# Moving rows of rotated attention queries between partitions: 32 small transfers become 32 copies on ScalarE

## The chip, the cores and the metric

One core of a Trainium2 chip runs the whole program. TensorE (PE) multiplies and transposes, VectorE (DVE), ScalarE (ACT) and GpSimd (POOL) do the elementwise work, and SyncE (SP) issues most of the transfers (DMAs). Each engine runs its own instructions in order and waits for the others by semaphores. The metric is the device time of one execution in microseconds (us); lower is better.

## The reference

A trunk of two layers, each over 1024 tokens of width 1024. A layer is a normalisation with conditioning, one wide input projection, three groups of heads side by side (windowed attention, retention, gated linear attention), a gate on each, and one output projection that is added to x.

```python
h = rms_norm(x, pre_gain) * (1.0 + scale) + shift
proj = h @ w_in
(aq, ak, av, ag, rq, rk, rv, rg, gq, gk, gv, gg, ga) = jnp.split(proj, IN_SPLITS, axis=-1)
aq = apply_rotary(aq.reshape(B, S, ATTN_HEADS, HEAD_DIM), positions, rope_freq)
ak = apply_rotary(ak.reshape(B, S, ATTN_KV_HEADS, HEAD_DIM), positions, rope_freq)
a_out = sliding_window_attention(aq, ak, av, sinks) * jax.nn.silu(ag)
...
def apply_rotary(x, positions, inv_freq):
    ...
    x1, x2 = jnp.split(x.astype(jnp.float32), 2, axis=-1)
    out = jnp.concatenate([x1 * cos - x2 * sin, x2 * cos + x1 * sin], axis=-1)
```

The change concerns `aq` alone: 8 query heads of 64 numbers, each rotated as two halves of 32.

## The kernel before

**Matrix products.** Activations and weights are split into a high and a low part, and each projection is three passes over 8 blocks of 128 input columns, 24 matmuls for one PSUM tile. Weights come in blocks of 256 columns ("units") through five staging buffers `st`, are split by ACT, DVE and POOL into an arena, and are multiplied from there. Three PSUM banks (`mm`) serve the projections; five (`aux`) serve, in turn, everything else: scores, transposes, attention values.

**The order of the work.** PE runs in the order in which the program is written (`manual_schedule` for PE): while projections are emitted, a written-out clock `clk` and a table of latencies `L` decide after which matmul the next piece of a waiting job (scores, transposes, values) is put in. So PE always has projection matmuls to run while softmax and the like pass through the other engines. The instructions of the other engines and of the transfer queues are put in order by the framework, by its own estimates; exchanging an instruction there can move neighbours.

**Queries.** `attn_rot` is called four times in a layer: for half `hf` of the tokens (512 each) and for key head `g`. Each call projects transposed queries of four heads, so that features lie on partitions and 512 tokens in a row. Two PSUM tiles, c = 0 and 1, hold the first and the second rotary halves: 32 partitions for each head. DVE multiplies each by cosine and sine (L867, L868; the tables come from DRAM by `t<-tabS`), then forms u[0] and u[1] (L870, L871), the rotated first and second halves. For the scores a head's 64 features have to lie together, the first half right beside the second: ACT copies u[j] to q[j] whole (L874), and then, for each j and r, 32 partitions of the other tile are put over the wrong quarter of q[j] (L877). That last step changes partitions (to 0, 32, 64 or 96 from another of these), and is done by 32x512 transfers on SP's queue, SBUF to SBUF, 64 KB each: 4 in a call, 16 in a layer, 32 in all. They are seen as `t<-t` in the profile. Afterwards `split_later` splits q on ACT (L835) and DVE (L836) into `mx`, which PE multiplies with the keys `kT` (`attn_scores`).

**Softmax.** `attn_turn` brings scores from PSUM into `smx` by ACT (L145, the previous block) and DVE (L934, the current block under the causal mask), reduces (L936), takes exponentials on ACT (L939), the reciprocal on DVE (L942), and scales on POOL (L943). PE transposes `smx` (L176), ACT copies the transposes out (L145, `t<-aux`), POOL masks a second version (L954), and PE forms the values. ACT copies these out (L145 again, `t<-aux`), SP stores them to DRAM (`aoS<-t`), and once two blocks of tokens of a half are there they come back as `t<-aoS` for the gate (L1445).

In layer 0 the modulation of the next layer is computed beside this: DVE accumulates rows of `w_mod` (L367), each from its own staging buffer.

Of the kernel before, what the change touches and what calls it, by code (L numbers as in the profile page):

```python
# [13 lines left out]
AF = mybir.ActivationFunctionType  # L14
# [5 lines left out]
S = 1024  # L20
# [69 lines left out]
def trunk(ctx: ExitStack, tc: tile.TileContext, ins, cst, out):  # L90
    nc = tc.nc
    V, A, G, T = nc.vector, nc.scalar, nc.gpsimd, nc.tensor
# [16 lines left out]
    def t2(dt=F32):  # L109
        return gp.tile([P, 512], dt, tag="t2", name=nm("t2"), bufs=B2)  # L110
# [10 lines left out]
    def mm():  # L121
        return ps.tile([P, 512], F32, tag="mm", name=nm("mm"), bufs=MMB)
# [4 lines left out]
    def f(ap):  # L127
        return ap.bitcast(F32)
# [11 lines left out]
    def eng(k):  # L140
        return G if EN[k] == "G" else V

    def copy(k, dst, src):
        if EN[k] == "A":
            A.activation(dst, src, AF.Copy)  # L145
        else:
            V.tensor_copy(dst, src)

    def dma(k, dst, src):
        {"S": nc.sync, "A": A, "P": G}[EN[k]].dma_start(dst, src)  # L150

# [31 lines left out]
    def job(gen):  # L183
        jobs.append([clk[0], None, gen])
# [21 lines left out]
    def pump():  # L206
        moved = True
        while moved:
            moved = False
            for j in list(jobs):  # L210
                r = ready(j)
                if r is not None and r <= clk[0]:
                    step(j)
                    moved = True
                    break
# [251 lines left out]
    def load(l, name, first=None, kcs=range(KT // 2)):  # L467
# [116 lines left out]
    def pre(l, t, xt, early=False, soon=False):  # L584
# [9 lines left out]
        with ExitStack() as es:  # L594
# [99 lines left out]
    def mix_tile(dt=F32R):  # L694
        return gp.tile([P, 2, KT, P], dt, tag="mx", name=nm("mx"), bufs=2)
# [142 lines left out]
    def split_later(mq, q, name):  # L838
        yield lat("aq6", name[1])
        for j in range(2):  # L840
            split(mq[:, 0, j], mq[:, 1, j], q[j])
        flag(name, lat("aq2", name[1]))
# [13 lines left out]
    def attn_rot(l, hf, g, w_):  # L856


        sn, cs = t2(), t2()
        for s, d in ((0, sn), (1, cs)):  # L860
            nc.sync.dma_start(d.rearrange("p (s n) -> p s n", s=2),
                              tabS[2 * hf:2 * hf + 2, :, s, :].rearrange("s p n -> p s n"))
        u, w = [t2(), t2()], [t2(), t2()]
        for c in range(2):
            pm = mm()
            project_T(pm, l, hf, w_, c * P)
            V.tensor_tensor(u[c], pm, cs, ALU.mult)  # L867
            V.tensor_tensor(w[1 - c], pm, sn, ALU.mult)  # L868
            pump()
        V.tensor_tensor(u[0], u[0], w[0], ALU.subtract)  # L870
        V.tensor_tensor(u[1], u[1], w[1], ALU.add)  # L871
        q = w
        for j in range(2):
            A.activation(q[j], u[j], AF.Copy)  # L874
            for r in range(2):
                dst, src = 64 * r + 32 * (1 - j), 64 * r + 32 * j
                dma("qst", q[j][dst:dst + 32], u[1 - j][src:src + 32])  # L877
        mq = mix_tile().rearrange("p a k q -> p (a k q)").rearrange("p (a j n) -> p a j n", a=2, j=2)
        kv[(hf, g)] = mq
        job(split_later(mq, q, ("q", l, hf, g)))  # L880
# [46 lines left out]
    def attn_turn(l, held, sms):  # L927
        for t, n, sm, pss in sms:
            for r in range(2):
                pv = pss[r][:, 0:2 * n].rearrange("p (j c n) -> p j c n", j=2, n=P)  # L930
                sv = sm[:, r:4:2, 0:128]
                if t > 0:
                    copy("sprev", sv, pv[:, :, 0, :])
                V.copy_predicated(sv, curmask.unsqueeze(1).to_broadcast((P, 2, P)), pv[:, :, n // P - 1, :])  # L934
            mx = small(4)
            V.tensor_reduce(mx, sm, AX.X, ALU.max, negate=True)  # L936
            sums = small(4)
            for h in range(4):
                A.activation(sm[:, h, :], sm[:, h, :], AF.Exp, bias=mx[:, h:h + 1],  # L939
                             accum_out=sums[:, h:h + 1])  # L940
            rs = small(4)
            V.reciprocal(rs, sums)  # L942
            eng("pn").tensor_tensor(sm[:, :, 0:128], sm[:, :, 0:128], rs.unsqueeze(2).to_broadcast((P, 4, P)), ALU.mult)  # L943
        yield lat("aq3", l)
        for t, n, sm, pss in sms:
            pp = aux()
            for h in range(4):
                transp(pp[:, h * P:(h + 1) * P], sm[:, h, 0:128], ident)
            pf = t2()
            copy("pf0", pf, pp)  # L950
            parts = [(held[("vp", t)], pf)]
            if t > 0:
                pr = t2()
                G.affine_select(h4(pr), h4(pf), [[0, 4], [1, P]], ALU.is_ge, 0.0, base=0, channel_multiplier=-1)  # L954
                parts.append((held[("vd", t)], pr))
            held[("parts", t)] = parts
# [356 lines left out]
    def layer(l):  # L1313
# [140 lines left out]
        for hf in range(2):  # L1454
            for g in range(2):
                attn_rot(l, hf, g, unit(l, f"aq{g}"))
                pump()
                if hf:
                    load(l, ("o3", "ag1")[g])
# [46 lines left out]


B2, B1, BS, BST, MMB, SMB = 12, 8, 11, 5, 3, 6
EN = {"qst": "S", "smh": "S", "sml": "S", "sm0": "S", "sm1": "S", "lao": "S", "sao": "S", "lmix": "S", "ssg": "S", "lsg": "S", "ssr": "S", "lsr": "A", "lx": "S", "sx": "A", "lw": "S", "lwm": "S", "whi0": "V", "whi1": "A", "whi2": "A", "whi3": "A", "wlo0": "V", "wlo1": "G", "wlo2": "V", "wlo3": "G", "xn0": "V", "xn1": "V", "hlo0": "G", "hlo1": "V", "rot0": "V", "rot1": "V", "rdec": "V", "kslo": "V", "qslo": "V", "vlo": "G", "kT": "A", "qT": "A", "sprev": "A", "pn": "G", "pf0": "A", "aoc": "A", "hng": "V", "mh": "A", "gso": "V", "mg": "V", "mgl": "V", "rT": "A", "rv": "A", "gv": "A", "gk": "A", "ak0": "V", "ak1": "V", "ak2": "V", "ak3": "V", "kd0": "G", "kd1": "G", "kd2": "G", "kx1": "G", "kx2": "G", "kx3": "V", "kx4": "V", "qb": "G", "stx": "V"}
TURN = ("AV", "AV")  # L1510
L = {"tt1": 5.71, "tt2": 6.96, "tb1": 28.02, "tb2": 0.05, "pf3": 12.62, "pf1": 6.69, "pf2": 4.0, "mod1": 4.3, "mod2": 2.4, "mod3": 17.69, "mod4": 5.8, "mod5": 0.09, "mod6": 0.05, "pre1": 7.43, "kv1": 8.84, "kv2": 2.31, "aq1": 7.17, "aq7": 7.95, "ag1": 5.62, "aq2": 2.4, "aq6": 6.2, "aq3": 11.35, "aq4": 7.54, "aq5": 4.01, "hn1": 8.14, "hn2": 3.76, "gz1": 10.47, "gz2": 13.49, "gl1": 4.43, "gd3": 16.57, "gc1": 1.21, "gc2": 1.95, "gc3": 0.65, "gc4": 3.27, "gc6": 3.2, "gc5": 4.23, "rc1": 0.73, "rc2": 2.11, "rc3": 1.31, "rc4": 2.84, "fin1": 11.68, "lay1": 0.05, "mod2@1": 2.23, "mod3@1": 16.46, "mod5@1": 3.78, "mod6@1": 3.24, "pre1@1": 10.18, "kv1@1": 3.37, "kv2@1": 0.05, "aq1@1": 5.95, "aq7@1": 6.81, "ag1@1": 8.3, "aq2@1": 2.07, "aq6@1": 9.39, "aq3@1": 11.0, "aq4@1": 6.32, "aq5@1": 1.76, "hn1@1": 10.35, "hn2@1": 3.59, "gz1@1": 3.83, "gz2@1": 12.55, "gl1@1": 17.99, "gd3@1": 15.63, "gc1@1": 1.6, "gc2@1": 1.95, "gc3@1": 0.47, "gc4@1": 1.87, "gc6@1": 0.05, "gc5@1": 1.38, "rc1@1": 0.12, "rc2@1": 3.46, "rc3@1": 2.6, "rc4@1": 5.99, "fin1@1": 9.35, "lay1@1": 1.23, "gc7": 0.81, "gc7@1": 0.33, "tb0": 0.05, "mod7": 1.0, "mod7@1": 1.0}
CHUNK = 7
# [51 lines left out]
```

## Time and profile before

| | |
|---|---|
| time, median of 3 runs | 972.73 us (972.31 to 973.64) |
| profiled execution | 971.16 us, of it 969.4 us from its first to its last instruction |
| granted TensorE clock | 0.996 |
| PE | busy 951.3 us, 98% of the span |
| DVE, ACT, POOL | 640.2, 410.1, 272.5 us (66%, 42%, 28%) |
| first to last `L874` | 300.2 to 809.8 us: in layer 0 the four calls lie at 300 to 346, in layer 1 at 764 to 810 |

A row of the timeline gives the start in us, the duration, engine, line, operation, output and inputs, and how many instructions are merged; in brackets the engine's idle time before it and what ended it. SPq is the transfer queue of SyncE: the duration there is that of issuing, not of the transfer.

### The profile page before, as it was taken

How to read it: one execution, taken by the hardware profiler on the slowest of the kernel's cores; microseconds unless marked ns; L12 is line 12 of the kernel's file. 1: busy time of each engine (PE TensorE's matmuls, PEld its weight loads, DVE VectorE, ACT ScalarE, POOL GpSimd, SP SyncE). 2: the span in 40 equal slices, each digit the busy share in tenths (PEclk: the TensorE clock that was granted, in tenths of full speed). 3: DMA queues.
4: the chain of work that ended last, by engine and by line, in shares of the span. 5: the costliest groups of instructions: out<-in, count | busy, mean ns of one | idle time of the engine just before them, and what ended most of it. 6: DMA issues, size and time to landing. Idle time of an engine off the chain costs nothing.

```text
span 969.4 us, 18061 instructions
## 1 busy us (share of the span) xinstructions
PE 951.3 (98%) x6513; PEld 829.4 (86%) x6513; DVE 640.2 (66%) x1525; ACT 410.1 (42%) x1119; POOL 272.5 (28%) x323
## 2 busy tenths in 40 slices
PE   6999999999999999999999999999999999999997
PEld 1799999989998877878889999998999887777886
DVE  6886857777777777655586485686776577763332
ACT  2777312354422666622455531134652166761111
POOL 3243011533430344511242110144423034441000
PEclk9999999999999999999999999999999999999999
DMA  9943314624335355677455160253222333555871
GB/s 313 320 146 110 111 56 129 187 77 112 115 102 150 98 168 180 218 242 237 172 166 172 50 180 22 83 155 92 80 86 77 120 88 105 158 174 174 261 238 65
DMA packets 124293, 140.30 MB, mean 145 GB/s; under 512 B 12734, under 2 KB 95528, under 8 KB 124204
## 3 DMA queue, kind: packets, MB, share of 16 engines
q1 hardware_dynamic: 116204, 127.43, 42.9%
q10 hardware_dynamic: 8000, 11.72, 3.4%
q8 instruction: 51, 0.84, 0.4%
q14 instruction: 38, 0.31, 0.1%
HBM read 102.42 MB, written 34.60 MB: 141 GB/s over the span
## 4 chain that ended last, share of the span: by engine, by line
PE 86%; DMA 7%; DVE 3%; issue 2%; POOL 1%; ACT 0%; SPq 0%; DVEq 0%; ACTq 0%; POOLq 0%
PE mm L161 67%; PE aux L161 15%; PE aux L176 4%; DMA wm<-in_w_mod_dram 2%; DMA t<-in_x_dram 1%; DMA st<-in_w_in_dram 1%; DMA xk<-in_x_dram 1%; DMA t<-aoS 1%; DMA st<-in_w_mod_dram 1%; POOL sm L529 1%; DVE acc L367 0%; DVE t L1292 0%; POOL arena L491 0%; DVE t L624 0%; DMA c_ident<-cst_ident_dram 0%
## 5 line engine op out<-in xcount | busy, mean ns | idle before, releaser
L161 PE MATMUL mm<-arena,arena 128*128 128x256 f32 (+2 forms) x1896 | 303.0, 315 | 1.4 <-ACT arena L628 0.7
L161 PE MATMUL mm<-arena 128*128 128x256 f32 (+2 forms) x1824 | 294.7, 317 | 0.0
L161 PEld LDWEIGHTS mm<-arena,arena 128*128 128x128 f32 x1896 | 261.8, 188 | 24.6 <-ACT arena L628 1.2
L161 PEld LDWEIGHTS mm<-arena 128*128 128x128 f32 x1824 | 255.4, 191 | 22.0 <-issue 1.2
L161 PE MATMUL mm<-arena,mx 128*128 128x512 f32 (+1 forms) x744 | 168.7, 386 | 0.0
L161 PEld LDWEIGHTS mm<-arena,mx 128*128 128x128 f32 x744 | 135.6, 188 | 29.1 <-issue 1.5
L529 POOL TENSOR_TENSOR sm<-sm,mhalf 128x4 f32<-128x4 f32 (+1 forms) x60 | 51.8, 863 | 294.8 <-DVE sm L528 285.3
L491 POOL TENSOR_TENSOR arena<-st,arena 128x512 fp32r<-128x512 f32 x55 | 80.3, 1467 | 91.3 <-ACT arena L145 34.7
L145 ACT ACTIVATE t<-aux 128x512 f32<-128x512 f32 (+1 forms) x96 | 48.7, 521 | 106.4 <-PE aux L176 44.9
L943 POOL TENSOR_TENSOR smx<-smx,sm 128x512 f32<-128x512 f32 x32 | 36.2, 1131 | 114.8 <-DVE sm L942 111.4
L491 DVE TENSOR_TENSOR arena<-st,arena 128x512 fp32r<-128x512 f32 x65 | 62.3, 969 | 4.7 <-PE mm L161 2.6
L145 ACT ACTIVATE arena<-st 128x512 fp32r<-128x512 f32 x82 | 48.5, 626 | 29.0 <-PE mm L161 13.0
L1247 ACT ACTIVATE t<-mm 128x512 f32<-128x512 f32 x30 | 17.9, 597 | 92.2 <-PE mm L161 40.3
L939 ACT ACTIVATE smx<-smx,sm 128x129 f32<-128x129 f32 x128 | 50.0, 393 | 14.0 <-DVE sm L936 13.9
L1248 DVE TENSOR_TENSOR t<-mm,modg 128x512 f32<-128x512 f32 x30 | 20.6, 689 | 48.6 <-ACT t L1247 48.5
L367 DVE SCALAR_TENSOR_TENSOR acc<-st,c_act,acc 128x512 f32<-128x512 f32 x60 | 47.3, 788 | 7.5 <-DMA st<-in_w_mod_dram 6.8
L1292 DVE SCALAR_TENSOR_TENSOR t<-t,sm,t 128x512 f32<-128x512 f32 x32 | 25.9, 846 | 39.7 <-DMA t<-xs 20.8
L176 PE MATMUL aux<-c_ident,t 128*128 128x128 f32 x288 | 45.5, 278 | 2.9 <-DVE t L602 2.9
L176 PEld LDWEIGHTS aux<-c_ident,t 128*128 128x128 f32 x288 | 34.9, 144 | 7.3 <-DVE t L602 4.2
L934 DVE COPY_PREDICATED smx<-c_curmask,aux 128x256 f32<-128x256 int32 x64 | 25.5, 447 | 15.0 <-ACT smx L145 10.4
L990 ACT ACTIVATE t<-aux 128x256 f32<-128x256 f32 x32 | 12.2, 382 | 54.1 <-PE aux L161 26.8
L995 DVE TENSOR_TENSOR t<-aux,sm 128x256 f32<-128x256 f32 x32 | 13.6, 425 | 30.8 <-POOL sm L529 30.8
(214 smaller groups left out, 1300.9 us busy)
## 6 DMA issues: line engine op xcount, KB each, us to landing
st<-in_w_in_dram SPq DMA_DIRECT2D x96, 256.0 KB
st<-in_w_mod_dram SPq DMA_DIRECT2D x64, 256.0 KB
mx<-mixS SPq DMA_DIRECT2D x30, 512.0 KB
mixS<-t SPq DMA_DIRECT2D x64, 128.0 KB
st<-in_w_out_dram SPq DMA_DIRECT2D x32, 256.0 KB
mixS<-t SPq DMA_DIRECT2D x32, 256.0 KB
wm<-in_w_mod_dram SPq DMA_DIRECT2D x12, 512.0 KB
t<-in_x_dram SPq DMA_DIRECT2D x24, 256.0 KB
```

The lines of the kernel that those rows point to most:

```text
L145: A.activation(dst, src, AF.Copy)
L161: T.matmul(dst, lhsT, rhs, start=start, stop=stop)
L176: T.transpose(dst, src, idn)
L367: V.scalar_tensor_tensor(acc, wt, c_act[:, k:k + 1], acc, ALU.mult, ALU.add)
L491: i = (G if first == 0 and kc in LOG else V if first == 0 else eng(f"wlo{kc}")).tensor_tensor(wt[:, 1, 2 * kc:2 * kc + 2, 0:256], st, f(hi ...
L529: after[2] = G.tensor_tensor(r, r, mhalf[:, :w], ALU.pow)
L934: V.copy_predicated(sv, curmask.unsqueeze(1).to_broadcast((P, 2, P)), pv[:, :, n // P - 1, :])
L939: A.activation(sm[:, h, :], sm[:, h, :], AF.Exp, bias=mx[:, h:h + 1], accum_out=sums[:, h:h + 1])
L943: eng("pn").tensor_tensor(sm[:, :, 0:128], sm[:, :, 0:128], rs.unsqueeze(2).to_broadcast((P, 4, P)), ALU.mult)
L1247: A.activation(yg, pm, AF.Square, accum_out=ss[:, nh:nh + 1])
L1248: V.tensor_tensor(yg, pm, modg[l][:, 512 * nh:512 * nh + 512], ALU.mult)
L1292: V.scalar_tensor_tensor(xt[j], yg[j], r, xt[j], ALU.mult, ALU.add)
```

## The change

The new helper `move` issues a transfer, an ACT copy or a copy on another engine, by its entry in the table `EN`. The four moves of a call have entries of their own, and all are set to ACT. Source, destination and shape (32x512, f32) stay.

```diff
+    def move(k, dst, src):
+        if EN[k] in "SP":
+            dma(k, dst, src)
+        elif EN[k] == "A":
+            A.activation(dst, src, AF.Copy)
+        else:
+            eng(k).tensor_copy(dst, src)
...
             for r in range(2):
                 dst, src = 64 * r + 32 * (1 - j), 64 * r + 32 * j
-                dma("qst", q[j][dst:dst + 32], u[1 - j][src:src + 32])
+                move(f"qst{2 * j + r}", q[j][dst:dst + 32], u[1 - j][src:src + 32])
...
-EN = {"qst": "S", ...
+EN = {"qst0": "A", "qst1": "A", "qst2": "A", "qst3": "A", ...
```

All lines behind the helper stand 8 lines further down (L874 is L882, L934 is L942, L367 is L375, L145 stays; the new copies are L153). PE's order of instructions is the same in both kernels. On the other engines the order changes near the eight calls only. Three places follow, all at the fourth call of layer 0 (the half from token 512 on, g = 1).

ACT, before and after, from the whole copies to the softmax of the next blocks:

```order
L874 ACTIVATE t_769_4238<-t_767_4236 128x512
L874 ACTIVATE t_768_4237<-t_766_4235 128x512
L145 ACTIVATE t_804_4453<-aux_4444 128x512
L145 ACTIVATE smx_4456<-aux_4460 128x2x128
L145 ACTIVATE smx_4456<-aux_4461 128x2x128
```

```order
L882 ACTIVATE t_769_4238<-t_767_4236 128x512
L882 ACTIVATE t_768_4237<-t_766_4235 128x512
L153 ACTIVATE t_769_4238<-t_766_4235 32x512
L153 ACTIVATE t_768_4237<-t_767_4236 32x512 x2
L153 ACTIVATE t_769_4238<-t_766_4235 32x512
L145 ACTIVATE t_804_4453<-aux_4444 128x512
L145 ACTIVATE smx_4456<-aux_4460 128x2x128
```

The four new copies stand ahead of the copy of the values out of PSUM (`t_804`) and of the scores (`smx_4456`).

DVE, at the mask of these scores (L934, then L942). `acc<-st` is the accumulation for the modulation:

```order
L367 SCALAR_TENSOR_TENSOR acc_4496<-st_4747,c_act,acc_4496 128x512
L934 COPY_PREDICATED smx_4456<-c_curmask,aux_4460 128x2x128
L934 COPY_PREDICATED smx_4456<-c_curmask,aux_4461 128x2x128
L273 COPY sm_4494<-aux_4492 128x16
L936 TENSOR_REDUCE sm_4507<-smx_4456 128x4
L934 COPY_PREDICATED smx_4474<-c_curmask,aux_4478 128x2x128
L836 TENSOR_TENSOR mx_4402<-t_768_4237,mx_4402 128x512
L836 TENSOR_TENSOR mx_4402<-t_769_4238,mx_4402 128x512
L907 COPY smx_4770<-sink_436 128x4
L907 COPY smx_4788<-sink_436 128x4
L367 SCALAR_TENSOR_TENSOR acc_4496<-st_4806,c_act,acc_4496 128x512
```

```order
L375 SCALAR_TENSOR_TENSOR acc_4496<-st_4747,c_act,acc_4496 128x512
L375 SCALAR_TENSOR_TENSOR acc_4496<-st_4806,c_act,acc_4496 128x512
L942 COPY_PREDICATED smx_4456<-c_curmask,aux_4460 128x2x128
L942 COPY_PREDICATED smx_4456<-c_curmask,aux_4461 128x2x128
L281 COPY sm_4494<-aux_4492 128x16
```

The accumulation of `st_4806` has moved ahead of the masks of the scores.

SP's queue, from the last rows of `w_mod` to the values that come back for the gate:

```order
L150 DMA st_4747<-in_w_mod_dram 128x512
L150 DMA t_768_4237<-t_767_4236 32x512 x2
L150 DMA t_769_4238<-t_766_4235 32x512 x2
L150 DMA st_4806<-in_w_mod_dram 128x512
L150 DMA aoS<-t_804_4453 128x2x256
L150 DMA st_4839<-in_w_out_dram 128x2x256
L150 DMA st_4843<-in_w_out_dram 128x2x256
L150 DMA st_4847<-in_w_out_dram 128x2x256
L150 DMA st_4851<-in_w_out_dram 128x2x256
L150 DMA st_4855<-in_w_out_dram 128x2x256
L150 DMA t_830_4560<-aoS 128x4x128
```

```order
L158 DMA st_4747<-in_w_mod_dram 128x512
L158 DMA st_4806<-in_w_mod_dram 128x512
L158 DMA st_4839<-in_w_out_dram 128x2x256
L158 DMA st_4843<-in_w_out_dram 128x2x256
L158 DMA st_4847<-in_w_out_dram 128x2x256
L158 DMA st_4851<-in_w_out_dram 128x2x256
L158 DMA aoS<-t_804_4453 128x2x256
L158 DMA st_4855<-in_w_out_dram 128x2x256
L158 DMA t_830_4560<-aoS 128x4x128
```

The four moves are gone, and the store of the values (`aoS<-t_804`) has moved behind four loads of weights.

More of the change, by code (lines that the diff above doesn't have):

```diff
@@ L1508 @@
 B2, B1, BS, BST, MMB, SMB = 12, 8, 11, 5, 3, 6
-EN = {"qst": "S", "smh": "S", "sml": "S", "sm0": "S", "sm1": "S", "lao": "S", "sao": "S", "lmix": "S", "ssg": "S", "lsg": "S", "ssr": "S", "lsr": "A", "lx": "S", "sx": "A", "lw": "S", "lwm": "S", "whi0": "V", "whi1": "A", "whi2": "A", "whi3": "A", "wlo0": "V", "wlo1": "G", "wlo2": "V", "wlo3": "G", "xn0": "V", "xn1": "V", "hlo0": "G", "hlo1": "V", "rot0": "V", "rot1": "V", "rdec": "V", "kslo": "V", "qslo": "V", "vlo": "G", "kT": "A", "qT": "A", "sprev": "A", "pn": "G", "pf0": "A", "aoc": "A", "hng": "V", "mh": "A", "gso": "V", "mg": "V", "mgl": "V", "rT": "A", "rv": "A", "gv": "A", "gk": "A", "ak0": "V", "ak1": "V", "ak2": "V", "ak3": "V", "kd0": "G", "kd1": "G", "kd2": "G", "kx1": "G", "kx2": "G", "kx3": "V", "kx4": "V", "qb": "G", "stx": "V"}
+EN = {"qst0": "A", "qst1": "A", "qst2": "A", "qst3": "A", "smh": "S", "sml": "S", "sm0": "S", "sm1": "S", "lao": "S", "sao": "S", "lmix": "S", "ssg": "S", "lsg": "S", "ssr": "S", "lsr": "A", "lx": "S", "sx": "A", "lw": "S", "lwm": "S", "whi0": "V", "whi1": "A", "whi2": "A", "whi3": "A", "wlo0": "V", "wlo1": "G", "wlo2": "V", "wlo3": "G", "xn0": "V", "xn1": "V", "hlo0": "G", "hlo1": "V", "rot0": "V", "rot1": "V", "rdec": "V", "kslo": "V", "qslo": "V", "vlo": "G", "kT": "A", "qT": "A", "sprev": "A", "pn": "G", "pf0": "A", "aoc": "A", "hng": "V", "mh": "A", "gso": "V", "mg": "V", "mgl": "V", "rT": "A", "rv": "A", "gv": "A", "gk": "A", "ak0": "V", "ak1": "V", "ak2": "V", "ak3": "V", "kd0": "G", "kd1": "G", "kd2": "G", "kx1": "G", "kx2": "G", "kx3": "V", "kx4": "V", "qb": "G", "stx": "V"}
 TURN = ("AV", "AV")
```

## The prediction

> **What bounds the kernel now.** I read the page first, then the busy times of the stretches in which the change acts, then PE's timeline inside them.
>
> ```profile
> PE 951.3 (98%) x6513; PEld 829.4 (86%) x6513; DVE 640.2 (66%) x1525; ACT 410.1 (42%) x1119; POOL 272.5 (28%) x323
> ...
> PE 86%; DMA 7%; DVE 3%; issue 2%; POOL 1%; ACT 0%; SPq 0%; DVEq 0%; ACTq 0%; POOLq 0%
> ```
>
> PE is busy 98% of the span, and the chain that ended last runs through PE for 86% of it; ACT and SP's queue have 0% there. An average can hide a stage with another limit, so the stages themselves:
>
> ```profile
> core 0: us, PE busy (x) PEld busy (x) DVE busy (x) ACT busy (x) POOL busy (x), PEclk, DMA share, GB/s
> 290.00:350.00 60.00, 60.00 (x355) 47.84 (x353) 45.97 (x89) 29.88 (x92) 17.57 (x16) 1.00 0.44 127
> 350.00:370.00 20.00, 19.50 (x115) 15.23 (x114) 13.67 (x32) 12.86 (x47) 6.38 (x7) 1.00 0.61 184
> 750.00:830.00 80.00, 80.00 (x472) 64.17 (x471) 53.70 (x104) 41.56 (x128) 22.22 (x23) 1.00 0.34 103
> ```
>
> The eight calls lie in the first and third row. PE shows no gap in either, at the full clock. Only behind the calls of layer 0, from 350 to 370, are 0.5 us free. Since PE's order is the same in both kernels, the end moves only by what PE waits more or less. How much waiting may hide inside "busy" is seen in the distance from the start of a group to the start of the next:
>
> ```profile
> 308.34 1.64 PE L161 MATMUL aux<-kT,mx 64*128 64x128 f32 x24
> 309.91 8.45 PE L161 MATMUL mm<-arena 128*128 128x512 f32 x36
> 318.29 1.69 PE L161 MATMUL aux<-kT,mx 64*128 64x256 f32 x24
> ...
> 336.96 8.62 PE L161 MATMUL mm<-arena,arena 128*128 128x512 f32 x36
> 345.50 0.65 PE L161 MATMUL aux<-t,va 128*64 128x256 f32 x4
> ...
> 349.17 1.20 PE L161 MATMUL mm<-arena,arena 128*128 128x512 f32 x4
> 350.39 1.06 PE L176 MATMUL aux<-c_ident,smx 128*128 128x128 f32 x8
> ...
> 362.81 0.66 PE L176 MATMUL aux<-c_ident,smx 128*128 128x128 f32 x4
> 363.94 0.63 PE L176 MATMUL aux<-c_ident,smx 128*128 128x128 f32 x4 [0.47 <-DVE smx L934]
> ```
>
> From 309.91 to 318.29 are 8.38 us for 36 matmuls, 0.233 us each: I take that as the pace without waits. From 336.96, 36 take 8.54, 0.15 more. From 349.17, four take 1.22 where 0.93 is due: a hidden wait of 0.29. The transposes at 362.81 and 363.94 lie 1.13 apart, where four of eight in 1.06 us need about 0.43: a wait of 0.70, of which the profile shows 0.47. With some ten groups in these stretches and 0 to 0.15 in most, about 2 us is all that PE could win if every wait vanished.
>
> By the Trainium skill (Perfetto Trace Analysis, Identifying the Most-Contended Engine) the busy share of matmuls is no good measure of how near PE is to its limit. The 0.29 us in a stretch called 100% busy agrees with it.
>
> **What is removed, and what replaces it.** ACT waits for the transfers ahead of the split of q,
>
> ```profile
> ACT mx L835 <- DMA t<-t: 14.6, 5, 4.2
> ```
>
> (the view of waits: total, times, longest), and at the first call, on SP's queue and on ACT:
>
> ```profile
> 300.84 2.65 SPq L150 DMA_DIRECT2D t<-t  x4
> ```
>
> ```profile
> 300.18 1.24 ACT L874 ACTIVATE t<-t 128x512 f32<-128x512 f32 x2 [3.51 <-DVE t L871]
> 305.60 1.16 ACT L835 ACTIVATE mx<-t 128x512 fp32r<-128x512 f32 x2 [4.18 <-DMA t<-t]
> ```
>
> So 14.6 us of ACT's waiting go, and 32 issues on SP's queue (2.65 us for four here). For the new copies no row has the shape; the nearest groups by shape (busy us, mean ns):
>
> ```profile
> L874 ACT ACTIVATE t<-t 128x512 f32<-128x512 f32 x16 | 9.9, 629 | 19.9 <-DVE t L871 17.1 <-DVE t L870 2.8
> L1121 ACT ACTIVATE mx<-t 32x256 f32<-32x256 f32 x32 | 13.2, 413 | 2.5 <-DVE t L1105 2.0
> L1007 ACT ACTIVATE t<-mm 128x256 f32<-128x256 f32 x32 | 11.9, 376 | 3.4 <-PE mm L161 3.4
> L335 ACT ACTIVATE row<-mm 1x512 f32<-1x512 f32 x2 | 1.2, 588 | 2.1 <-PE mm L161 2.1
> ```
>
> Partitions hardly matter: one partition of 512 takes 588 ns, and 32 of 256 take 1.10 times what 128 take. So a copy lies between 588 and 629 x 1.10 = 692 ns; I take L874's 629, the same width. 32 of them are 20.1 us more work for ACT. Back to back they overlap (two L835 in 1.16 us), so four cost 2.3 us in a row (2.1 to 2.8). At the first call L874 ends at 301.42; L835 can then start at 303.7, not 305.60. Nobody gains: PE reaches the first scores at 308.34 without a gap as it is. I cost this at 0; the cover is the projection matmuls, and without them the 1.9 us a call would be won.
>
> **What the copies delay.** Where ACT did not wait for the transfers at once, the 2.3 us fall on the instructions behind. The tightest place is the fourth call, in layer 0 and in layer 1:
>
> ```profile
> 345.34 0.63 ACT L874 ACTIVATE t<-t 128x512 f32<-128x512 f32 x1 [1.13 <-DVE t L870]
> 347.56 0.60 ACT L145 ACTIVATE t<-aux 128x512 f32<-128x512 f32 x1 [1.58 <-PE aux L161]
> 348.45 1.10 ACT L145 ACTIVATE smx<-aux 128x256 f32<-128x256 f32 x3 [0.29 <-PE aux L161]
> 810.82 0.60 ACT L145 ACTIVATE t<-aux 128x512 f32<-128x512 f32 x1 [0.43 <-PE aux L161]
> ```
>
> ```profile
> 815.18 1.03 PE L176 MATMUL aux<-c_ident,smx 128*128 128x128 f32 x8
> ```
>
> In layer 0 the copies end at 345.97 + 2.3 = 348.3 and the values leave PSUM at 348.9, not 348.16; the scores follow until 349.3. DVE reaches their mask at 349.79, so this still fits. In layer 1 the copies push 810.82 by at most 2.3, to 813.1, and the scores behind it to 814.5; the bank that the first of them frees is wanted by the second four transposes, near 815.6. It fits by about 1 us. Price: 0.
>
> **What DVE's new order delays.** Here the change reaches PE:
>
> ```profile
> 337.88 0.48 DVE L365 TENSOR_SCALAR acc<-st,c_act 128x512 f32<-128x512 f32 x1
> ...
> 346.62 3.26 DVE L367 SCALAR_TENSOR_TENSOR acc<-st,c_act,acc 128x512 f32<-128x512 f32 x4
> 349.79 0.78 DVE L934 COPY_PREDICATED smx<-c_curmask,aux 128x256 f32<-128x256 int32 x2
> ...
> 352.88 0.75 DVE L367 SCALAR_TENSOR_TENSOR acc<-st,c_act,acc 128x512 f32<-128x512 f32 x1
> ```
>
> The accumulation at 352.88 now stands ahead of the masks at 349.79. It costs 0.75 alone, 0.79 in a row (3.17 us for four from start to start): I take 0.75. PE's transposes at 350.39 need the bank that the first mask frees (its end, some 350.18, explains the 0.29), so they start at 351.1: **+0.75 us**. Its data should be in: its transfer no longer stands behind the four moves (issued at 346.00, below), and its buffer, five loads back, was read at 337.88.
>
> **The wait at 363.94.** DVE's mask was late there because it stood behind the gate (L1445), which waited for a transfer; DVE's rows, then SP's queue:
>
> ```profile
> 360.11 0.69 DVE L1445 SCALAR_TENSOR_TENSOR t<-t,t 128x512 f32<-128x512 f32 x1 [4.62 <-DMA t<-aoS]
> ...
> 818.78 0.69 DVE L1445 SCALAR_TENSOR_TENSOR t<-t,t 128x512 f32<-128x512 f32 x1 [1.36 <-DMA t<-aoS]
> ```
>
> ```profile
> 346.00 2.42 SPq L150 DMA_DIRECT2D t<-t  x4
> ...
> 349.14 0.41 SPq L150 DMA_DIRECT2D aoS<-t  x1
> 349.64 4.39 SPq L150 DMA_DIRECT2D st<-in_w_out_dram  x5
> 354.13 1.77 SPq L150 DMA_DIRECT2D t<-aoS  x2
> ...
> 813.33 0.54 SPq L150 DMA_DIRECT2D aoS<-t  x1
> 815.66 0.92 SPq L150 DMA_DIRECT2D t<-aoS  x2
> ```
>
> If the gate's data come no later than 360.11, a PE that is 0.75 late meets the mask just as it is freed: the wait of 0.70 is gone, **-0.7 us**. When do they come? The store now waits behind a fourth load of weights whose buffer the accumulation before 349.79 frees: issued near 350.4, not 349.14. The fifth load, which held back `t<-aoS` until 354.13, waits for the accumulation moved forward, so it goes at 351. The store lands 2.3 us after its issue if it goes like layer 1's (813.33 to 815.66), 6.0 if it goes like the load here (354.13 to 360.11): 352.7 to 356.4. The load then takes 3.1 (815.66 to 818.78) to 6.0. Arrival: 355.8 to 362.4, the middle 359.1. So it is in time, with 2.3 us of delay at worst.
>
> **The sum:** 971.16 of the profiled execution, 0 for ACT, +0.75, -0.70: 971.2, or 972.8 beside the median of 972.73, which lies 1.57 above that execution. I predict **972.8**.
>
> **Rivals.** *The waits were on the path.* If the 14.6 us that ACT waited, with SP's issues, held up the end, the time would be 958.1. Against it stand the 60.00 of 60 and 80.00 of 80 us. What can really be won is the 2 us of hidden waits above: 970.7. For it speaks that L835 comes earlier and the gate's data may too; against it that most of these waits lie at switches the change does not touch. Faster, 10%.
>
> *The store behind the weights.* If store and load both take the 6.0 us, the gate starts 2.3 us later, DVE holds masks and reciprocal behind it, and the transposes at 363.94 start 2.3 us later: 975.0. It counts as slower from an arrival near 362.1. For it speaks a stretch with 184 GB/s; against it that the loads go out earlier and spread. 6%.
>
> *Slow copies.* If changing partitions made an ACT copy dear, the slack at the fourth calls ends: 345.97 + 4d + 0.6 + 0.4 must not pass 350.5 (the masks, 0.75 later), so d above 0.9 us back to back. At 1.26, twice L874, two places lose 1.4 each: 975.6. L1121 speaks against it, if only in its width of 32 partitions. 4%.
>
> *Only one half of the sum happens:* -0.70 or +0.75 alone, 972.0 or 973.5; both are within what counts as no change.
>
> **How the numbers follow.** A measurement of this kernel tells about 0.2%, 1.9 us, from no change. No change 80%, faster 10%, slower 10%. The range goes from the hidden waits (970.7) plus a little, 971.0, to the late store, 975.0.
>
> **What would show it.** ACT's busy time rises by 20 us, with 32 rows of 32x512 near 0.63; the wait for `t<-t` is gone; PE's busy time and chain share stay. The transposes after the fourth call of layer 0 start some 0.7 us later against the four matmuls ahead of them; the wait before the second four, near 364, shrinks below 0.3; L1445 starts before 360. A PE gap over 1 us from 300 to 370 or 764 to 830, or copies over 0.9 us, would prove me wrong, as would an end that moves while PE's gaps there do not.

## The result, and the profile after

The change makes the kernel slower, by little: 975.01 us (median; 972.34 to 978.91) against 971.60 us (969.78 to 973.77) for the kernel before, a ratio of 1.0042 with a 95% interval of 1.0032 to 1.0051. Timed a second time it was 1.0037 (1.0023 to 1.0051). Predicted were 972.8 us and no change that can be measured. The profiled execution of the changed kernel took 974.2 us, its span is 972.5, 3.1 more than the span before.

The page of the changed kernel, busy times and the chain that ended last:

```profile
PE 950.4 (98%) x6513; PEld 828.8 (85%) x6513; DVE 638.1 (66%) x1525; ACT 430.2 (44%) x1151; POOL 269.4 (28%) x323
...
PE 89%; DMA 5%; DVE 2%; issue 2%; POOL 1%; ACT 0%; ACTq 0%; DVEq 0%; SPq 0%; POOLq 0%
```

Nothing here says where the time went: ACT works 20.1 us more and still has 0% of the chain, PE is busy as before. The same stretches as in the prediction, of the changed kernel, say it:

```profile
core 0: us, PE busy (x) PEld busy (x) DVE busy (x) ACT busy (x) POOL busy (x), PEclk, DMA share, GB/s
290.00:350.00 60.00, 58.49 (x332) 46.54 (x330) 44.09 (x90) 36.53 (x100) 15.53 (x15) 1.00 0.36 112
350.00:370.00 20.00, 19.01 (x131) 14.89 (x128) 15.42 (x33) 13.39 (x42) 4.65 (x7) 1.00 0.53 160
750.00:830.00 80.00, 80.00 (x482) 64.62 (x482) 51.91 (x110) 50.15 (x139) 20.60 (x21) 1.00 0.28 87
```

In layer 1 (last row) PE still has no gap. In layer 0 it now stands still for 1.5 us in the first row and 1.0 in the second, at the full clock. The view of waits, for PE from 290 to 430 us (total, times, longest):

```profile
PE aux L184 <- ACT t L145: 1.4, 2, 1.2
PE aux L184 <- DVE smx L942: 1.1, 2, 0.8
```

Before there was one row in its place, 0.5 us for a mask near 364. PE's timeline shows the places, first in the changed kernel, then in the kernel before at the third call and behind the wait near 364 (the matmuls between them are left out):

```profile
309.59 1.64 PE L169 MATMUL aux<-kT,mx 64*128 64x128 f32 x24
...
334.76 1.65 PE L169 MATMUL aux<-kT,mx 64*128 64x128 f32 x24
337.60 0.66 PE L184 MATMUL aux<-c_ident,smx 128*128 128x128 f32 x4 [1.19 <-ACT t L145]
338.58 0.65 PE L184 MATMUL aux<-c_ident,smx 128*128 128x128 f32 x4 [0.33 <-DVE smx L942]
339.07 0.95 PE L169 MATMUL aux<-c_ones,acc 128*128 128x1 f32 x8
...
350.30 1.70 PE L169 MATMUL aux<-kT,mx 64*128 64x256 f32 x24
352.23 0.23 PE L184 MATMUL aux<-c_ident,rows 16*128 16x16 f32 x1 [0.23 <-ACT t L145]
352.39 1.19 PE L169 MATMUL mm<-arena,arena 128*128 128x512 f32 x4
354.35 1.06 PE L184 MATMUL aux<-c_ident,smx 128*128 128x128 f32 x8 [0.77 <-DVE smx L942]
...
366.78 1.09 PE L184 MATMUL aux<-c_ident,smx 128*128 128x128 f32 x8
367.63 1.64 PE L169 MATMUL mm<-arena 128*128 128x512 f32 x6
```

```profile
335.09 1.22 PE L176 MATMUL aux<-c_ident,smx 128*128 128x128 f32 x8
336.14 0.95 PE L161 MATMUL aux<-c_ones,acc 128*128 128x1 f32 x8
...
364.32 1.87 PE L161 MATMUL mm<-arena 128*128 128x512 f32 x7
```

Where two executions are compared, only distances count, because the start differs: the first scores stand at 309.59 here, at 308.34 before. From them to the projection behind the transposes near 366 (367.63 here, 364.32 before) are 58.04 us; before they were 55.98. This distance is called the stretch below. The 2.06 us are +1.68 at the third call, +1.04 at the fourth, and -0.66 where the wait near 364 is gone. The prediction had the last of these and 0.75 of the second, and nothing at the third call.

**Why the third call.** ACT at the third call (the half from token 512 on, g = 0), in the changed kernel: the whole copies, the four new copies, the split, and the copy of the attention values out of PSUM (`t<-aux`, the value copy below):

```profile
331.62 0.63 ACT L882 ACTIVATE t<-t 128x512 f32<-128x512 f32 x1 [0.77 <-DVE t L879]
332.66 0.63 ACT L882 ACTIVATE t<-t 128x512 f32<-128x512 f32 x1 [0.41 <-DVE t L878]
333.32 2.56 ACT L153 ACTIVATE t<-t 32x512 f32<-32x512 f32 x4
335.91 1.15 ACT L843 ACTIVATE mx<-t 128x512 fp32r<-128x512 f32 x2
336.97 0.58 ACT L145 ACTIVATE t<-aux 128x512 f32<-128x512 f32 x1
```

and before:

```profile
328.26 1.15 ACT L874 ACTIVATE t<-t 128x512 f32<-128x512 f32 x2
332.94 1.15 ACT L835 ACTIVATE mx<-t 128x512 fp32r<-128x512 f32 x2 [3.54 <-DMA t<-t]
334.00 0.58 ACT L145 ACTIVATE t<-aux 128x512 f32<-128x512 f32 x1
```

The value copy ends at 337.55, and PE's transposes begin at 337.60: they need the bank that it empties. Taking off the 1.25 us of the start, the value copy comes 1.72 us later than before, although four copies on ACT (2.56) are faster than four transfers were (3.54 of waiting). The whole copies end 2.63 us later: 333.29 - 1.25 = 332.04 against 329.41. So the copies win back 0.9 us of a lateness that is there before they start. It comes from DVE. In the changed kernel:

```profile
326.30 0.18 DVE L950 RECIPROCAL sm<-sm 128x4 f32<-128x4 f32 x1 [1.08 <-ACT smx L947]
...
326.97 0.91 DVE L147 CAST arena<-st 128x512 fp32r<-128x512 f32 x1
327.80 1.26 DVE L915 COPY smx<-sink 128x4 f32<-128x4 f32 x1
328.98 0.68 DVE L499 TENSOR_TENSOR arena<-st,arena 128x512 fp32r<-128x512 f32 x1
...
329.74 0.65 DVE L875 TENSOR_TENSOR t<-mm,t 128x512 f32<-128x512 f32 x1
```

and before, where the cast and the L491 belonging to it stood ahead of that reciprocal, so that they were done while the exponentials ran:

```profile
322.71 0.41 DVE L147 CAST arena<-st 128x512 fp32r<-128x512 f32 x1
323.15 0.69 DVE L491 TENSOR_TENSOR arena<-st,arena 128x512 fp32r<-128x512 f32 x1
324.23 0.18 DVE L942 RECIPROCAL sm<-sm 128x4 f32<-128x4 f32 x1 [0.38 <-ACT smx L939]
...
325.54 0.68 DVE L867 TENSOR_TENSOR t<-mm,t 128x512 f32<-128x512 f32 x1
```

The products of the third call's queries (L875, before L867) start at 329.74 - 1.25 = 328.49, not at 325.54: 2.95 us late. Two things of the second call are in this. Its own copies on ACT put the exponentials (L947), and with them the reciprocal, 0.82 us later. And the framework's new order puts a cast and an addition behind the reciprocal that stood ahead of it, so that from the reciprocal to the products it takes 3.44 us and not 1.31: 2.13 us.

### The profile page after: what moved, and what is told of

It is laid out like the page before. It is cut to its first block, busy times and chain, and to the rows that moved or that the text cites. A ratio compares the mean times of both kernels' runs of the same rounds, so it can differ in the third digit from the quotient of the medians.

```text
span 972.5 us, 18019 instructions
## 1 busy us (share of the span) xinstructions
PE 950.4 (98%) x6513; PEld 828.8 (85%) x6513; DVE 638.1 (66%) x1525; ACT 430.2 (44%) x1151; POOL 269.4 (28%) x323
## 4 chain that ended last, share of the span: by engine, by line
PE 89%; DMA 5%; DVE 2%; issue 2%; POOL 1%; ACT 0%; ACTq 0%; DVEq 0%; SPq 0%; POOLq 0%
PE mm L169 70%; PE aux L169 15%; PE aux L184 4%; DMA wm<-in_w_mod_dram 2%; DMA st<-in_w_in_dram 1%; DMA t<-in_x_dram 1%; POOL sm L537 0%; DVE acc L375 0%; DMA posi<-in_positions_dram 0%; DMA rows<-in_pre_norm_gain_dram 0%; POOL arena L499 0%; DVE t L632 0%; ACT arena L636 0%; DMA gncol<-in_gla_norm_gain_dram 0%; DVE t L878 0%
## 5 line engine op out<-in xcount | busy, mean ns | idle before, releaser
L145 ACT ACTIVATE t<-aux 128x512 f32<-128x512 f32 (+1 forms) x96 | 48.8, 522 | 104.2 <-PE aux L184 45.7
L145 ACT ACTIVATE arena<-st 128x512 fp32r<-128x512 f32 x82 | 48.5, 625 | 29.1 <-PE mm L169 13.2
L947 ACT ACTIVATE smx<-smx,sm 128x129 f32<-128x129 f32 x128 | 50.0, 393 | 14.8 <-DVE sm L944 14.7
L375 DVE SCALAR_TENSOR_TENSOR acc<-st,c_act,acc 128x512 f32<-128x512 f32 x60 | 47.9, 798 | 6.9 <-DMA st<-in_w_mod_dram 6.2
L942 DVE COPY_PREDICATED smx<-c_curmask,aux 128x256 f32<-128x256 int32 x64 | 25.3, 446 | 17.2 <-ACT smx L145 10.8
```

The costliest lines, as they stand in the source:

```text
L375: V.scalar_tensor_tensor(acc, wt, c_act[:, k:k + 1], acc, ALU.mult, ALU.add)
```

## The experiments

**The change in layer 1 alone.** Does layer 1 cost anything?

```diff
-                move(f"qst{2 * j + r}", q[j][dst:dst + 32], u[1 - j][src:src + 32])
+                (move if l == 1 else dma)(f"qst{2 * j + r}" if l == 1 else "qst", q[j][dst:dst + 32], u[1 - j][src:src + 32])
```

> Copies on ACT in layer 1's four calls only; layer 0 keeps the transfers. Theory W (the loss is what PE waits for at the third and fourth call of layer 0, in the profile of the change 1.7 + 1.0 - 0.7 = 2.1 us): no loss, ratio 1.000 to 1.001, no PE wait over 0.2 us between 740 and 880. Rival E (every call costs, by more work on ACT, by the clock or by anything that no PE wait shows): half of the 0.42%, ratio near 1.002.

Measured: 972.04 us (970.30 to 973.15) beside 971.44, ratio 0.9999 (0.9990 to 1.0009). No PE wait of the view stands from 290 to 430 or from 740 to 880. Sixteen copies, 10 us of ACT's time, cost nothing that can be measured where their cover holds. One more thing is seen: the transposes that the wait of 0.47 split before run as one here, with the order of layer 0 untouched.

```profile
363.03 1.09 PE L184 MATMUL aux<-c_ident,smx 128*128 128x128 f32 x8
```

**The change in layer 0 alone** (the same edit with `l == 0`).

> Copies on ACT in layer 0's four calls only. Theory W: the whole loss, ratio 1.002 to 1.004; PE waits of 1.2 and 0.3 us at the transposes of the third call, of 0.2 and 0.8 at the fourth, as in the change. Rival E: half of the loss, near 1.002, with the other half in layer 1.

Measured: 974.26 us, ratio 1.0025 (1.0016 to 1.0034). The waits are those of the whole change, 1.4 and 1.1 us, at the same places, and the stretch from the first scores takes 58.05 us. The loss of the calls lies in layer 0.

**The third call of layer 0 alone** (the condition is `(l, hf, g) == (0, 1, 0)`): are its own copies enough for the wait of 1.19?

> Copies on ACT in the third call of layer 0 only. The order on DVE is then that of before. Theory W1 (the third call loses because the copies of the second call moved DVE's instructions, so that u came 2.1 us later): the copies end near 332.0, the values leave PSUM at 334.0 as before, no PE wait at 335. Rival W2 (the 2.6 us of four copies by themselves push the values' copy): PE waits about 1.2 us there.

Measured, one execution: 972.75 us, stretch 56.05. DVE's order is that of the kernel before, and on ACT

```profile
331.62 2.56 ACT L153 ACTIVATE t<-t 32x512 f32<-32x512 f32 x4
334.21 1.15 ACT L843 ACTIVATE mx<-t 128x512 fp32r<-128x512 f32 x2
335.80 0.60 ACT L145 ACTIVATE t<-aux 128x512 f32<-128x512 f32 x1 [0.44 <-PE aux L169]
```

ACT has the split done 0.44 us before PE delivers the values. The copies alone do not make the wait of 1.19. What this execution shows instead are two waits for masks, 0.42 us at 338.34 and 0.26 at 353.29, the second at the fourth call, whose rows are transfers here.

**The fourth call of layer 0 alone** (`(l, hf, g) == (0, 1, 1)`).

> Copies on ACT in the fourth call of layer 0 only. DVE's accumulation stands ahead of the masks here too. Theory: the transposes at 350.4 start 0.8 to 1.0 us later against the scores ahead of them, the wait of 0.7 near 364 goes, net about 0.3 us. Rival (the third call's delay made the fourth late): no later than before.

Measured, one execution: 971.58 us, stretch 56.10. The fourth call's two waits are there, a little shorter, without any change at the third:

```profile
349.70 0.23 PE L184 MATMUL aux<-c_ident,rows 16*128 16x16 f32 x1 [0.15 <-ACT t L145]
...
351.64 1.07 PE L184 MATMUL aux<-c_ident,smx 128*128 128x128 f32 x8 [0.58 <-DVE smx L942]
```

**The change, timed again beside the next ones.**

> The changed kernel itself, timed a second time beside the others, because its first ratio (1.0042) and that of the layer-0 part alone (1.0025) leave 1 to 1.7 us unexplained while layer 1 alone gave 0.9999. Theory N (one loss of 2 to 2.7 us in layer 0, the rest is spread between runs): ratio 1.002 to 1.003, and the same waits in the profile, 1.2 <- ACT t and 0.3 <- DVE smx at the third call, 0.2 and 0.75 at the fourth, no others. Rival (a second loss that needs both layers): the ratio stays at or above 1.004, and the profile has PE waits outside 300 to 370 that the layer-0 part does not have.

Measured: 976.17 us, ratio 1.0037 (1.0023 to 1.0051), the same waits and one of 0.15 us for a mask at 394.65, stretch 58.07. The ratio lies between what the two theories expected, and a wait of 0.15 us does not answer for it.

**Everything but the second call of layer 0**, whose rows stay transfers (`(l, hf, g) != (0, 0, 1)`).

> All copies on ScalarE except those of the second call of layer 0, which stay transfers. DVE's order at the third call is then that of the kernel before. Theory W1 (the copies of the second call moved other work ahead of the third call's products on DVE, and that is what makes its rows late): the wait of 1.2 us <- ACT t at the third call is gone, 0 to 0.5 us of a mask wait stay there, the fourth call keeps its 0.8 to 1.0, the wait near 364 stays gone (-0.66); together +0.2 to +0.9 us against before, ratio 1.000 to 1.0012. Rival W2 (the third call's own copies are enough): the 1.2 us stay, ratio 1.0020 or more. Against the whole change, timed beside it, W1 expects this kernel 1.5 to 2.5 us faster.

Measured: 972.71 us beside 971.91, ratio 1.0007 (0.9997 to 1.0017), stretch 56.23. At the third call there is no wait at all, though its copies run on ACT as in the change (2.57 us from 329.27); what is left are the fourth call's two:

```profile
PE aux L184 <- DVE smx L942: 0.7, 1, 0.7
PE aux L184 <- ACT t L145: 0.2, 1, 0.2
```

The second call's four copies, with the order on DVE that comes with them, are what makes the third call late: taking them out takes out 1.8 us of the stretch (58.04 to 56.23) and, timed side by side, 3.5 us of the medians.

**Narrow copies.** All copies on ScalarE, but only 16 of the 512 columns of each are copied, so the rotation of the other columns is left incomplete. The order of DVE at the third call stays that of the change, but for one addition; the work is gone.

```diff
-                move(f"qst{2 * j + r}", q[j][dst:dst + 32], u[1 - j][src:src + 32])
+                move(f"qst{2 * j + r}", q[j][dst:dst + 32, :16], u[1 - j][src:src + 32, :16])
```

> All copies on ScalarE as in the change, but each copies only 16 of the 512 columns (so the other columns of the rotated half rows are left as they were). PE, SP and POOL have the same order as the change, DVE at the third call too but for one addition (L499) that moves by a row or two. It takes the length of the copies away and leaves the order. A narrow copy should take 0.15 to 0.25 us, four in a row 0.6 to 1.0 in place of 2.56. Theory L (lateness from the order, 1.7 to 2.1 us, and 2.56 us of copies add up): the value copy at the third call comes 1.6 to 1.9 us earlier, the 1.2 us wait <- ACT t is gone or below 0.3; the mask waits <- DVE smx (0.33 and 0.75), which hang on DVE's order, stay; time 1.2 to 1.6 us below the change. Rival O (the order alone does it): the 1.2 us stay within 0.3, time as the change. Rival C (it is the copies' length everywhere): the mask waits go too, time as before.

Measured: 972.61 us, ratio 1.0006 (0.9997 to 1.0015), stretch 56.23. Four copies in a row take 0.90 us, and the value copy waits for PE again. The first fence is ACT at the third call, the second DVE from the second call's reciprocal to the third call's products, the third DVE at the fourth call, where the accumulations stand ahead of the mask as in the change:

```profile
331.53 0.63 ACT L882 ACTIVATE t<-t 128x512 f32<-128x512 f32 x1 [0.41 <-DVE t L878]
332.19 0.90 ACT L153 ACTIVATE t<-t 32x16 f32<-32x16 f32 x4
...
335.41 0.60 ACT L145 ACTIVATE t<-aux 128x512 f32<-128x512 f32 x1 [1.14 <-PE aux L169]
```

```profile
325.17 0.18 DVE L950 RECIPROCAL sm<-sm 128x4 f32<-128x4 f32 x1 [1.08 <-ACT smx L947]
...
328.61 0.65 DVE L875 TENSOR_TENSOR t<-mm,t 128x512 f32<-128x512 f32 x1
```

```profile
348.35 4.23 DVE L375 SCALAR_TENSOR_TENSOR acc<-st,c_act,acc 128x512 f32<-128x512 f32 x5
352.49 0.78 DVE L942 COPY_PREDICATED smx<-c_curmask,aux 128x256 f32<-128x256 int32 x2
```

PE's waits at the third call are both gone, that of 0.33 too, which was expected to stay. DVE's new order alone does not make that one; what it hangs on stays open, because under the old order the third call alone showed 0.42 us there, and everything but the second call none. At the fourth call the wait for the mask stays, 1.05 us: it does not need the copies' length. (It is longer by about what ACT's wait of 0.23, now gone, had covered.) The whole copies of the third call end at 332.16 - 1.78 = 330.38 (its first scores are 1.78 later than in the first profile of the kernel before), 0.97 late, where the change has them 2.63 late: 1.66 us of that lateness is the length of the copies ahead. It is all in the reciprocal, which comes at 325.17 - 1.78 = 323.39, 0.84 earlier than in the kernel before (ACT has no transfers to wait for and little to copy), where the change has it 0.82 later. From the reciprocal to the products it takes 3.44 us here as in the change: the new order's 2.13 us do not depend on the copies' length. So the order is the larger part of the 2.95 us. It makes no wait here, where the short copies give back 0.84 of it and the third call's own copies are short too. Whether either part alone would make PE wait was not tried. An estimate from these rows: the value copy was 1.72 late and PE waited 1.19, so 0.53 us of lateness costs nothing; without the 0.82, 0.90 would be left, a wait of some 0.4 us. The fourth call's wait for the mask is the order alone, its 0.23 the length alone.

**The kernel before, profiled again.**

> The kernel before, unchanged, profiled a second time: is the wait near 364 (0.47 in the profile, 0.70 by the distance of the transposes) a fixed part of the kernel before, or chance? Fixed: the first transposes of that place stand 1.1 us ahead of the second again. Chance: both run as eight in 1.06 us, as in the kernel that has the change in layer 1 alone, and the distance from 308 to 368 is 0.7 shorter than in the first profile, so that the change loses 2.7 us against it and not 2.0. The start up to the first scores at 308.3 may differ by up to 2 us either way, as it did among the profiles so far.

Measured, one execution: 972.30 us, first scores at 310.93, stretch 55.48. The wait near 364 isn't there:

```profile
365.51 1.14 PE L176 MATMUL aux<-c_ident,smx 128*128 128x128 f32 x8
```

Nor is it there with layer 1 alone, so it comes and goes: the change has nothing sure to win there, and its cost in the stretch is larger than the first pair of profiles says.

**The change, three more executions**, for what the stretch doesn't explain of the timed loss.

> The changed kernel, one more profile. Open: the timed loss (3.5 to 4 us) is larger than the 2.0 to 2.6 us that the stretch from 308 to 368 shows in two profiles, both taken at a mean granted clock of 0.996 to 0.997; the timed runs of the change with 0.994 or less lie near 977, those with 0.996 or more near 974. Theory K (the rest is granted clock: some executions have a throttled stretch more): the 60 us of the calls again take 58.0 to 58.1; if this run has 0.994 or less, its time is 976 to 978, and the extra 2 to 3 us stand in slices below the full clock, with no new PE wait there. Rival P (another wait that comes and goes): the extra stands as a PE wait outside 300 to 370.

> As the look before: the same kernel, to have more than one chance of an execution at a clock of 0.994 or less. Theory K: calls 58.0 to 58.1 us, any extra in slices below the full clock. Rival P: any extra as a PE wait at the full clock.

> As the two looks before, the same kernel a last time. Theory K: calls 58.0 to 58.1 us, any extra in slices below the full clock. Rival P: any extra as a PE wait at the full clock.

Measured: 975.06, 974.02 and 974.87 us, stretches of 57.82, 57.74 and 57.81, the wait of 1.19 in each, and no low clock from the calls to PE's last matmul. None of the three had the clock of 0.994 or less that was looked for (0.997, 0.995, 0.997).

**Two copies on ScalarE, two on VectorE.** The whole computation is done; DVE's order is again that of the change.

```diff
-EN = {"qst0": "A", "qst1": "A", "qst2": "A", "qst3": "A", ...
+EN = {"qst0": "A", "qst1": "V", "qst2": "A", "qst3": "V", ...
```

> Two of the four copies of a call on ScalarE and two on VectorE; the whole computation is done. DVE's order beside the copies is that of the change but for small moves (L499, L844). Theory L (lateness of the rows, 2.1 us by DVE's order, and 2.56 us of copies in ACT's row add up at the third call): ACT has 1.28 us there, the value copy comes 1.0 to 1.3 us earlier, the 1.2 us wait <- ACT t falls to 0 to 0.3. The fourth call's wait of 0.75 for the mask stays (the accumulation is still ahead) and may grow by DVE's own copies, 0.4 to 0.6 each, to 0.75 to 1.5. Together 0.3 to 1.3 us below the change, ratio to before 1.001 to 1.003. Rival (DVE, 66% busy, is the worse place): the masks come 1 us later at every call, waits <- DVE smx at the third and fourth call of 1 us or more each, time as the change or above.

Measured: 975.38 us beside 972.27, ratio 1.0034 (1.0021 to 1.0047), stretch 59.23. The third call is cured, as expected from halving ACT's copies: no wait for the value copy, 0.18 for a mask. The time is not below the change, as it was expected to be. At the fourth DVE pays: its own copies (1.07 us for two) stand ahead of the accumulations, and PE waits 2.02 us. Behind that wait came something that no theory had:

```profile
354.86 1.85 PE L184 MATMUL aux<-c_ident,smx 128*128 128x128 f32 x8 [2.02 <-DVE smx L942]
356.36 6.77 PE L169 MATMUL mm<-arena,arena 128*128 128x512 f32 x24
```

```profile
352.00:355.00 3.00, 0.98 (x5) 0.53 (x4) 2.90 (x6) 0.99 (x2) 0.00 (x0) 0.99 0.70 227
355.00:358.00 3.00, 3.00 (x12) 2.71 (x12) 2.87 (x10) 2.19 (x10) 0.18 (x1) 0.50 0.90 296
```

From 355 to 358 the granted clock (the third figure from the end) stood at one half; finer windows have it at 0.50 from 355.0 to 358.4 and at 1.00 behind. From the eight transposes to the next projection are 1.50 us, where the change has 0.82, and the 24 matmuls after it take 6.60 from start to start, where it has 5.67: 1.6 us lost in this execution on top of the wait.

**Four more executions of the change**: does its own wait of 1.19 do the same now and then, and is that the rest of the loss?

> The changed kernel, one more profile, now with a sharper theory. In the profile of the run with copies on two engines the granted clock stood at 0.50 from 355 to 358, right behind a PE wait of 2.02 us, and the matmuls after it took 0.9 us longer. Theory K2: PE's waits at the third or fourth call (1.2, 0.8 us) now and then do the same in the change, and that is the part of the timed loss beyond 2 to 2.6 us. In such an execution slices of 0.5 stand between 336 and 364, 3 to 4 us long, and the stretch from the first scores to the last transposes takes 59.5 to 60 us in place of 58.0 to 58.1. Rival P: the stretch stays at 58.0 to 58.1 in every look and the extra stands elsewhere.

> The same kernel and the same question: theory K2, slices of half clock between 336 and 364 and a stretch of 59.5 to 60 us in some looks; rival P, 58.0 to 58.1 in every look.

> The same kernel and the same question: theory K2, slices of half clock between 336 and 364 and a stretch of 59.5 to 60 us in some looks; rival P, 58.0 to 58.1 in every look.

> The same kernel and the same question, a last look: theory K2, slices of half clock between 336 and 364 and a stretch of 59.5 to 60 us in some looks; rival P, 58.0 to 58.1 in every look.

Measured: 975.70, 976.75, 976.11 and 976.24 us, stretches of 58.09, 58.24, 57.74 and 57.81. The half clock doesn't occur in the calls in any of them, so in the profiles that theory finds no support. What differs is the time before the first call. The longest of these executions is also the one at a clock of 0.993: its first scores came at 311.74, and the clock stood at 0.50 in its window from 20 to 24. But a low clock near the start is not the change's own: in the first profile of the kernel before it stood at 0.50 from 18.9 to 22.3 and from 36.0 to 39.3, with the first scores at 308.34.

**The account over all profiles.** From the first scores to the projection behind the transposes near 366, and the time of the first scores, in us:

| kernel | timed ratio | stretch | against 55.6 | first scores |
|---|---|---|---|---|
| before, and layer 1 alone (its layer 0 is the same) | 1, 0.9999 | 55.98, 55.48, 55.44 | 0 | 308.34, 310.93, 308.44 |
| third call alone, fourth call alone | - | 56.05, 56.10 | +0.4, +0.5 | 310.52, 308.81 |
| all but the second call | 1.0007 | 56.23 | +0.6 | 308.10 |
| narrow copies | 1.0006 | 56.23 | +0.6 | 310.12 |
| layer 0 alone | 1.0025 | 58.05 | +2.4 | 309.83 |
| the change, nine executions | 1.0042, 1.0037 | 57.74 to 58.24, mean 57.93 | +2.3 | 309.59 to 311.74, mean 310.60 |
| two engines | 1.0034 | 59.23 | +3.6 | 310.53 |

For every kernel but the change itself the stretch accounts for the timed ratio within its interval (0.1% is 0.97 us); that of the two engines has the 1.6 us at half clock in it, which need not be in each of its executions. The change is timed at +3.4 to +4.3 us by medians, and 2.3 of it lie in the calls: that is below the first interval (1.0032 to 1.0051) and just inside the second (1.0023 to 1.0051). From the calls to PE's last matmul nine executions of it take 599.2 us on average, the three of the first row 599.0. In the profiles the rest, some 1.4 us, stands before the first call: the mean of the first scores is 310.60, against 309.2 over the six executions of the rows above "narrow copies", and 309.5 over all nine of other kernels. Until the first call the order of the instructions is the same on every engine in both kernels, and the two executions of the kernel before differ by 2.6 us. Whether the change has a part in this or the sample is too small stays open.

The timed executions, of which only the mean clock is recorded, add something else. At a clock of 0.997 the change takes 974.4 us (mean of 11) and the kernel before 972.2 (mean of the 24 timed beside the experiments): 2.3 us, what the stretch shows. But 10 of 32 executions of the change had 0.994 or less, with a mean of 977.1 us, and only 1 of 59 of the kernel before. So part of the timed loss goes with more time at a low clock. Nine of these ten were not profiled, so where the low clock stood in them, and whether PE's new waits bring it on, is not shown.

## Why the prediction was wrong

**What bounds the kernel** was right: PE's order is fixed, and in the calls the end moved by what PE waited. So was the reading that 14.6 us of ACT's waiting and 32 issues on SP's queue were worth nothing: layer 1 alone, with half of the moves, gives 0.9999. The hidden wait of 0.29 ends at 350.39, in the row of 19.50 of 20 and not in one of 100%; but of the 1.22 us around it the profile counts 1.20 as busy.

**The price of a copy** was right alone, not in a row. It was 629 ns in the groups of the changed kernel, the figure taken, and ACT's busy time rose by 20.1 us. But two copies don't overlap as two splits do:

```profile
L153 ACT ACTIVATE t<-t 32x512 f32<-32x512 f32 x32 | 20.1, 629 | 0.6
```

Four in a row take 2.56 us, 0.64 from start to start, not 2.3; the range of 2.1 to 2.8 held. The Trainium skill (ScalarE: Activation LUTs, What ACT_TABLE_LOAD costs) has ACT instructions back to back overlap by about 93 ns. The two splits agree (1.15 us for two of 0.63); these copies don't, and the narrow ones don't either (four of 16 columns in 0.90 us).

**"Nobody gains" at the first call** was right: the split starts at 305.27 - 1.25 = 304.0, 1.6 us earlier than before, and PE doesn't notice.

**"The tightest place is the fourth call"** is the step that failed. The fourth calls were worked through and the price for ACT put at 0 for the whole kernel; the second and the third call of layer 0 were never looked at, in ACT's rows or in DVE's order. There the change costs 1.68 us, where the sum has nothing. The second call had no slack for its exponentials, the reordered rows on DVE there were as plain in the two orders as the one that was priced, and the bank that the third call's value copy empties was the next one that PE wanted. The means of the prediction were enough to see it: a copy of 0.63, a row of waiting instructions behind it, and the PE group that takes the bank.

**"In layer 0 ... this still fits"** was off by 0.3. The values were to start leaving PSUM at 348.3; in the change they do at 351.58 - 2.93 = 348.65 (2.93 is the start plus the third call). The prediction checked the masks and overlooked the transpose of `rows` at 349.01, which wants the bank earlier: 0.23 us of wait, 0.30 in distance.

**"In layer 1 ... fits by about 1 us"**: right, 80.00 us of 80.

**+0.75 for the accumulation moved ahead of the masks**: right. From the four matmuls to the transposes are 354.35 - 352.39 = 1.96 us, where 1.22 stood before: +0.74. That it is the order, and not the copies, the narrow copies show.

**-0.70 for the wait near 364**: the wait went, by 0.66, and the gate's wait fell from 4.62 to 2.47 us. The store was issued at 353.50 - 2.93 = 350.6, near the 350.4 of the forecast. But the second profile of the kernel before doesn't have this wait, nor has the kernel with layer 1 alone. The gain was read from one execution and was luck; against the usual one the sum should have been +0.75, and with the 1.68 and the 0.30, 2.7. Over all profiles it is 2.3.

**The rivals.** "The waits were on the path": refuted by layer 1. "The store behind the weights": the store did go later, but the gate came in time, so its 975.0 is the measured time by luck. "Slow copies" had the right kind of mechanism, copies that delay the value copy until PE wants its bank, with the wrong condition: it asked for copies above 0.9 us, and 0.64 was enough at a call that was already late. Its 975.6 came near the time by luck as well. Of the signs that the prediction named, "a PE gap over 1 us from 300 to 370" is the one that spoke.

## What to carry to other kernels

Where a step is done at several places, each of them has to be priced against the buffer that PE wants next, and the slack that the step ahead has already eaten counts: here the copies were free at five of eight places, cost 0.3 us at one, and cost 1.7 us at one only because of what the call ahead of it had done. Each row that the framework reorders is a term of the sum, not only those beside the edit. A wait seen in one profile is worth a second profile before it is counted as a gain.

## What the runs showed that was not expected

A PE wait of 2.02 us was followed by half the clock: 0.50 for the 3.4 us behind it, with 1.6 us lost. Waits of 1.19 and 0.77 us, some 17 us apart, were not followed by it in nine profiled executions. By the Trainium skill (TensorE: Matmul & The Clock Gate, Part 1: The HAM clock gate) the clock falls after an idle window of about 3.4 us, and windows run free. The measured length of the low stretch agrees with such a window; the wait doesn't, since in the 3 us from 352 to 355 PE was still busy for 0.98. It was one execution, so whether the wait was the cause, and how often a wait of 2 us does this, is open.

Four narrow copies show what a copy that changes partitions costs on ACT: 0.225 us each for 16 columns and 0.64 for 512, that is 0.84 ns for a column and about 0.21 us for each instruction.
